# Low and high half of a weight block in one tile, sums of blocks stored in both halves, column sums by transposition, and a ring of 49 tiles

## The chip, the cores and the metric

The kernel runs on one core of a Trainium2 chip. The metric is the device time of one execution in microseconds (us). Before the change it is 2611.89 us, the median of three runs (2609.43 to 2612.32).

## The reference, cut to what matters

One layer is computed for 2112 tokens (2048 of a prompt, 64 of a sample with states of their own), model width 1024, all in float32.

```python
h = rms_norm(x, g_pre)
vA, bA, cA, zA, q, f, iv, zB, gA, gB = split_cols(h @ w_in)        # 1024 x 10240
u_ext = concat([conv_hist, cA * vA])
yA = (silu(zA) * bA * causal_conv3(u_ext, conv_w)) @ w_a_out       # path A
fg = lb + (1 - lb) * sigmoid(f)                                    # path B: 8 heads, chunks of 64
S_new, o = hgrn2_scan(S0, silu(q) * K_B**-0.5, 1 - fg, iv, log(fg))
o = o * rsqrt(mean(o * o) + EPS)
yB = (o * g_onorm * silu(zB)) @ w_b_out
out = (sigmoid(gA) * yA + sigmoid(gB) * yB) @ w_o
x = x + rms_norm(out, g_post)
x = x + (p @ w_ple_proj) * sigmoid(rms_norm(x, g_ple) @ w_ple_gate)
```

## The kernel before, in words

**Blocks.** Tokens are worked on in three blocks of 704, each in two halves of 352, which is the moving size of nearly every matmul. Features lie on partitions. For each block the program runs `path_b` (eight heads of the scan with their four in-projections), `path_a` (the convolution path), the merge with W_A and W_B, W_O, the norms and the gate W_G. Products that belong to the next block fill gaps.

**Split floats.** A float32 operand is split in a high part `hi` (a cast on ScalarE) and a low part `lo = x - hi` (a subtraction on VectorE), both in `split` at L188. A product is three matmuls: hi with the high part of the tokens, hi with their low part, lo with their high part (L363, L364, L365 in `sgroup`; L496 to L498 in `in_turn`; L529 to L531 in `mm3`).

**Weights.** A weight comes in blocks of 128x512 floats (256 KB, `w_blk`). SyncE (SP) loads a block into one of 5 `raw` tiles (L198). The first time a block is used, ScalarE casts and VectorE subtracts (L188), and SP stores the low part to DRAM (`low`, L225). Later, ScalarE casts again (L218), and SP loads the stored low part (L219) into one of 4 `lo` or 3 `s` tiles. There are 4 `hi` tiles.

**Seven products for eight.** Large products are done as groups of 2x2 blocks with seven products (`PRODUCTS`, `sgroup`); four of the seven weight operands are sums of blocks, S1 to S4. In block 0 `combined` makes them on VectorE (L297) in an `s` tile and stores the sum (L276) and its low part (L225). From block 1 on `kept_w` loads a sum into `raw`, casts it, and loads its low part. The sums of the late weights are made ahead by `prepare_sums`: GpSimd (POOL) loads four blocks into ring tiles (L320), VectorE makes four sums (L337, L339, L341, L343), POOL stores each sum (L326); each is split by a cast and a subtraction, and POOL stores the low part (L329). For W_A and W_B this runs in block 0's merge (`ahead=True`, eight groups, the low part through the three `s` tiles); for W_O in block 1 and for W_G in block 2 it runs a group at a time beside `path_a`.

**Order.** Program order with priorities sets each engine's order; tiles come from pools in turn, and who takes a tile waits for all readers of the one that lay there, a storing DMA too. `hooks` is a list of small pieces of work; one is taken after each product of a group. Column sums: `col_rstd` adds 128 rows of squares by matmuls with a column of ones (L620), three tiles of a half; VectorE scales them (L591), POOL takes the power (L593), `spread` turns the result back by transposing matmuls (L604). The ring has 52 tiles of 128x708 floats for everything else.

Of the kernel before, what the change touches and what calls it, by code (L numbers as in the profile page):

```python
# [35 lines left out]
CUT = 1344  # L36
BN = 704
HN = BN // 2
NB = TOK // BN
RING = 52  # L40
# [5 lines left out]
def plan():  # L46


    out = []
    for t0 in range(0, TOK, BN):  # L50
        runs, groups = [], []
        for lo, hi, sample in ((0, CUT, False), (CUT, CUT + DEC, True), (CUT + DEC, TOK, False)):
            a, b = max(lo, t0) - t0, min(hi, t0 + BN) - t0
# [7 lines left out]
        halves = [dict(t0=t0 + o, off=o, n=HN) for o in (0, HN)]  # L61
        out.append(dict(t0=t0, n=BN, runs=runs, npair=npair, parts=parts, groups=groups, segs=halves, last=t0 + BN == TOK))
# [20 lines left out]
def hybrid_step(  # L83
# [35 lines left out]
    def rt(n=BN, dt=F32):  # L119
        t = ring.tile([P, BN + 4], dt, tag="r", name=nm("r"))  # L120
        return t if n is None else t[:, :n]

    def hf(n=HN):
        return ring.tile([P, HN + 32], F32, tag="hf", name=nm("hf"), bufs=HALVES)[:, :n]
# [4 lines left out]
    def ps_gemm():  # L129
        return psg.tile([P, 512], F32, tag="pg", name=nm("pg"))[:, :HN]  # L130

    def spill(kind, j):
        return dram.tile([P, BN], F32, tag=f"{kind}{j}", name=nm(kind), bufs=2)
# [4 lines left out]
    ones = const.tile([P, 1], F32, tag="ones", name="ones")  # L138
    V.memset(ones, 1.0)
# [6 lines left out]
    keep = const.tile([P, BN], F32, tag="keep", name="keep")  # L146
    atts = [
        const.tile([P, max(len(b["parts"][i]) for b in blocks), P], F32, tag=f"att{i}", name=f"att{i}") for i in range(NPART)
# [41 lines left out]
    def split_rt(src):  # L190
        hi, lo = rt(dt=F32R), rt(dt=F32R)
# [3 lines left out]

    def load_raw(src):
        raw = wp.tile([P, 4, P], F32, tag="raw", name=nm("raw"), bufs=5)
# [3 lines left out]
    lows, turn = {}, [0]  # L201

    def low_tile():

        turn[0] += 1
        if turn[0] % 7 in (1, 3, 5):
            return sum_tile(F32R)
        return wp.tile([P, 4, P], F32R, tag="lo", name=nm("lo"))

    def sum_tile(dt=F32):  # L210
        return wp.tile([P, 4, P], dt, tag="s", name=nm("s"), bufs=3)

    def split_w(raw, key=None, queue=SP):

        hi = wp.tile([P, 4, P], F32R, tag="hi", name=nm("hi"))
        if key in lows:
            lo = low_tile()
            A.copy(hi, raw)  # L218
            SP.dma_start(lo.bitcast(F32), lows[key])  # L219
            return hi, lo  # L220
        lo = wp.tile([P, 4, P], F32R, tag="lo", name=nm("lo"))
        split(raw, hi, lo)
        if key is not None:
            lows[key] = dram.tile([P, 4, P], F32, tag=f"lo{key}", name=nm("low"), bufs=1)
            queue.dma_start(lows[key], lo.bitcast(F32))  # L225
        return hi, lo

    def load_w(idx, anew=False):

        parts = []  # L230
        for half_ in range(2):
            raw = load_raw(w_blk[idx, half_])
            with tc.high_priority():
                unread = W_A <= idx < W_O and (idx % KB < KH or half_ == 0)
                parts.append(split_w(raw, None if anew or unread else (idx, half_)))
# [37 lines left out]
    def keep_sum(name, i1, s, queue):  # L273

        sums.setdefault(i1, {})[name] = dram.tile([P, 4, P], F32, tag=f"{name}_{i1}", name=nm(name), bufs=1)
        queue.dma_start(sums[i1][name], s)  # L276
        return split_w(s, (i1, name), queue)

    def kept_w(i1, i2, name, anew=False):

        keys = dict(A11=(i1, 0), A12=(i1, 1), A22=(i2, 1))
        if name in keys:
            return split_w(load_raw(w_blk[keys[name]]), None if anew else keys[name])
        return split_w(load_raw(sums[i1][name]), (i1, name))

    def combined(i1, i2, first):

        queue = SP if first else G
        with tc.high_priority():
            if not first and i1 in sums:  # L290
                return {n: kept_w(i1, i2, n) for _, n, _, _, _ in PRODUCTS}
            a11, a21, a22, a12 = (load_raw(w_blk[i, h]) for i, h in ((i1, 0), (i2, 0), (i2, 1), (i1, 1)))
# [16 lines left out]
    def prepare_sums(firsts, ahead):  # L309
# [4 lines left out]
        def tile_of(dt=F32):  # L314
            return rt(4 * P, dt).rearrange("p (k c) -> p k c", c=P)

        def load(i1, i2):
            out = [tile_of() for _ in range(4)]
# [4 lines left out]
        def keep(name, i1, s):  # L323
            sums.setdefault(i1, {})[name] = dram.tile([P, 4, P], F32, tag=f"{name}_{i1}", name=nm(name), bufs=1)
            lows[i1, name] = dram.tile([P, 4, P], F32, tag=f"lo{name}_{i1}", name=nm("low"), bufs=1)
            G.dma_start(sums[i1][name], s)  # L326
# [6 lines left out]
        for n, (i1, _) in enumerate(groups):  # L333
# [4 lines left out]
            keep("S1", i1, a22)  # L338
            V.tensor_tensor(a21, a11, a21, ALU.subtract)  # L339
            keep("S3", i1, a21)  # L340
            V.tensor_tensor(a11, a22, a11, ALU.subtract)  # L341
            keep("S2", i1, a11)
            V.tensor_tensor(a12, a12, a11, ALU.subtract)  # L343
# [5 lines left out]
    def sgroup(i1, i2, hc, sink, first, mid=None, by_k=False):  # L349
# [5 lines left out]
        def product(n, ks):  # L355
# [3 lines left out]
            hi, lo = w[block]  # L359
# [34 lines left out]
    def half(t, h):  # L394
        return t[:, h * HN : (h + 1) * HN]
# [15 lines left out]
    def plain_group(i1, i2, hs, sink, raws=None, between=None):  # L411
# [14 lines left out]
        def add(c, ks):  # L426
            for k in ks:
                hi, lo = w[c, k // KH]
# [41 lines left out]
    def in_turn(stages, operand):  # L470
# [10 lines left out]
        for i, (st, n) in enumerate(todo):  # L481
# [3 lines left out]
            for g in range(KH):  # L485
                i1, i2 = st["idx"] + g, st["idx"] + KH + g
                with tc.high_priority():
                    hi, lo = kept_w(i1, i2, IN_TURN[n][0], IN_TURN[n][0] in st["anew"])
# [37 lines left out]
    def mm3(ps, w, act, k, c, ks=range(KB)):  # L526
        hi, lo = w[k // 4]
# [19 lines left out]
    def gemm_late(idxs, act, segs, late):  # L547
# [3 lines left out]
        ks = [k for k in range(KB) if k != late] + [late]  # L551
# [55 lines left out]
    def spread_all(cols):  # L607

        rs = rt()
        for h in range(2):  # L610
            A.copy(half(rs, h), spread(cols[h], HN))
        return rs

    def col_rstd(acc, n):
# [3 lines left out]
        with placed():  # L618
            for i, o in tiles_of(n):
                T.matmul(pc[:, i : i + 1], acc[:, o : o + P], ones, start=True, stop=True)  # L620
        rstd_of(pc[:, : cols.shape[1]], cols, 1.0 / D)
# [19 lines left out]
    def load_x(bl, k):  # L641
        t = rt()
        G.dma_start(t, x_fm[k * P : (k + 1) * P, bl["t0"] : bl["t0"] + BN])
        return t

    def row_rstd(bl, out):

        out.extend(cols_tile(HN) for _ in bl["segs"])
        todo = [(cols, s["t0"] + o, i) for cols, s in zip(out, bl["segs"]) for i, o in tiles_of(HN)]
# [120 lines left out]
    def path_a(bl, hc, a, first, extra, ready=None):  # L770

        for j in range(KB):
            next(extra, None)
            n = bl["n"]
            pos = [r[0] + 2 * i for i, r in enumerate(bl["runs"])]
            hists = [hist_s if r[2] else hist_p for r in bl["runs"]]
            ct, u, conv = rt(), rt(None), rt()
# [4 lines left out]
            def times_u(h, v):  # L782
                for (o, ln, _), q in zip(bl["runs"], pos):
                    lo, hi = max(o, h * HN), min(o + ln, (h + 1) * HN)
                    if lo < hi:
                        V.tensor_tensor(
                            u[:, q + 2 + lo - o : q + 2 + hi - o], v[:, lo - h * HN : hi - h * HN], ct[:, lo:hi], ALU.mult
# [13 lines left out]
            for (o, ln, _), q, hist in zip(bl["runs"], pos, hists):  # L801
                d = conv[:, o : o + ln]
                A.mul(d, u[:, q : q + ln], cw[0][:, j : j + 1])
                for w in (1, 2):
                    V.scalar_tensor_tensor(d, u[:, q + w : q + w + ln], cw[w][:, j : j + 1], d, ALU.mult, ALU.add)
# [20 lines left out]
    def head_prep(bl, hc, hd, first, hs):  # L826
        n, npair = bl["n"], bl["npair"]
        nch, np1 = n // CH, npair * P
# [18 lines left out]
        qc = small.tile([P, 2, BN // CH], F32, tag="qc", name=nm("qc"))  # L847
        f, r = qc[:, 0, :nch], qc[:, 1, :nch]
        ka, kb, qx, vt, z = hf(HN + 32), rt(), rt(), rt(), rt()

        def scaled(after):
# [16 lines left out]
            two = kb[:, : 4 * P].rearrange("p (c q t) -> p c q t", q=4, t=CH)  # L868
            rest = kb[:, 4 * P : np1].rearrange("p (g c t) -> p g c t", c=2, t=CH)[:, :, 0, :]
# [632 lines left out]
```

## Time and profile before

| | |
|---|---|
| median of three runs | 2611.89 us |
| the profiled execution's own time | 2611.61 us |
| its span | 2609.9 us |
| granted TensorE clock, mean | 1.000 |
| TensorE (PE) busy | 2588.6 us, 99% |
| VectorE (DVE), ScalarE (ACT), GpSimd (POOL) busy | 64%, 59%, 15% |
| DMA queue of SP (q1), of POOL (q0), share of 16 engines | 65.4%, 17.0% |

Busy shares are means over the whole span. The waits of an engine name the instruction that waited and what released it. A window of the trace gives the busy time of each engine and the share of the 16 DMA engines in that stretch.

### The profile page before, as it was taken

The numbers are of one execution on the slowest core, as the hardware profiler recorded it, in microseconds if no ns is written. First come the engines' busy times: TensorE is split into PE (matmuls) and PEld (weight loads), VectorE is DVE, ScalarE is ACT, GpSimd is POOL, SyncE is SP. The second block draws the span as 40 slices with busy tenths as digits, with TensorE's granted clock in tenths as the row PEclk, the third lists the DMA queues.
The fourth block names the chain that finished last, engine by engine and source line by source line (L and its number), as shares of the span: only waits on it lengthen the run. The fifth ranks groups of instructions, "written<-read, shape, count | busy, mean of one in ns | idle before, by whom it ended". The sixth has DMA issues, their size and how long they took to land.

```text
span 2609.9 us, 47443 instructions
## 1 busy us (share of the span) xinstructions
PE 2588.6 (99%) x16562; PEld 2572.5 (99%) x16562; DVE 1667.1 (64%) x3232; ACT 1538.9 (59%) x2940; POOL 392.6 (15%) x722
## 2 busy tenths in 40 slices
PE   8999999999999999999999999999999999999999
PEld 8999999999999999999999999999999999999998
DVE  8778888888766555455545568553455544568756
ACT  6666665554434644677745556466667744555746
POOL 2000000200441212101112211021000101210220
PEclk9999999999999999999999999999999999999999
DMA  7687787898988997777789989599776789999977
GB/s 285 234 275 259 251 285 257 306 318 286 342 292 285 351 320 259 248 231 224 226 288 359 381 311 312 193 359 358 229 230 220 224 256 335 377 321 309 339 256 240
DMA packets 362672, 745.99 MB, mean 286 GB/s; under 512 B 44640, under 2 KB 49280, under 8 KB 362432
## 3 DMA queue, kind: packets, MB, share of 16 engines
q1 hardware_dynamic: 319680, 579.55, 65.4%
q0 software_dynamic: 42464, 163.37, 17.0%
q8 instruction: 130, 2.13, 0.3%
q14 instruction: 110, 0.90, 0.1%
q10 hardware_dynamic: 288, 0.05, 0.0%
HBM read 531.74 MB, written 211.04 MB: 285 GB/s over the span
## 4 chain that ended last, share of the span: by engine, by line
PE 89%; DMA 3%; DVE 2%; issue 2%; ACT 1%; POOL 1%; DVEq 0%; POOLq 0%; ACTq 0%; SPq 0%
PE pg L363 19%; PE pg L365 19%; PE pg L364 19%; PE pg L496 4%; PE pg L497 4%; PE pg L498 4%; PE pg L530 4%; PE pg L531 4%; PE pg L529 4%; PE pa L994 1%; PE pa L958 1%; PE pa L996 1%; PE pa L944 1%; DMA r<-w_blk 1%; DMA raw<-S 1%
## 5 line engine op out<-in xcount | busy, mean ns | idle before, releaser
L363 PE MATMUL pg<-r,hi 128*128 128x352 f32 x3304 | 1092.9, 331 | 4.6 <-DVE r L409 3.1
L364 PE MATMUL pg<-r,hi 128*128 128x352 f32 x3304 | 1067.6, 323 | 0.0
L365 PE MATMUL pg<-r,lo 128*128 128x352 f32 x2356 | 762.1, 323 | 1.2 <-DMA lo<-low 1.2
L218 ACT CAST hi<-raw 128x512 fp32r<-128x512 f32 x720 | 445.0, 620 | 499.8 <-PE pg L364 165.6
L363 PEld LDWEIGHTS pg<-r,hi 128*128 128x128 f32 x3304 | 622.2, 188 | 9.1 <-DVE r L409 3.2
L364 PEld LDWEIGHTS pg<-r,hi 128*128 128x128 f32 x3304 | 622.2, 188 | 0.0
L365 PEld LDWEIGHTS pg<-r,lo 128*128 128x128 f32 x2356 | 442.3, 188 | 1.8 <-DMA lo<-low 1.7
L365 PE MATMUL pg<-r,s 128*128 128x352 f32 x948 | 306.2, 323 | 0.1
L530 PE MATMUL pg<-r,hi 128*128 128x352 f32 x768 | 248.4, 324 | 0.0
L529 PE MATMUL pg<-r,hi 128*128 128x352 f32 x768 | 248.1, 323 | 0.0
L188 ACT CAST hi<-raw 128x512 fp32r<-128x512 f32 x218 | 134.6, 621 | 153.1 <-PE pg L364 53.5
L188 DVE TENSOR_TENSOR r<-r,r 128x352 fp32r<-128x352 f32 (+3 forms) x298 | 182.8, 637 | 62.7 <-ACT r L188 61.7
L497 PE MATMUL pg<-r,hi 128*128 128x352 f32 x672 | 217.3, 325 | 0.0
L496 PE MATMUL pg<-r,hi 128*128 128x352 f32 x672 | 213.6, 325 | 0.1
L531 PE MATMUL pg<-r,lo 128*128 128x352 f32 x656 | 211.9, 323 | 0.1
L188 ACT CAST r<-r 128x352 fp32r<-128x352 f32 (+3 forms) x298 | 162.2, 580 | 56.9 <-DVE r L1114 15.4
L188 DVE TENSOR_TENSOR lo<-raw,hi 128x512 fp32r<-128x512 f32 x218 | 149.4, 687 | 63.5 <-ACT hi L188 55.2
L365 PEld LDWEIGHTS pg<-r,s 128*128 128x128 f32 x948 | 178.4, 188 | 0.4 <-DMA s<-low 0.4
L188 ACT CAST hi<-s 128x512 fp32r<-128x512 f32 x160 | 98.5, 621 | 123.0 <-PE pg L364 105.8
L377 ACT COPY hf<-pg 128x352 f32<-128x352 f32 x354 | 157.1, 446 | 11.5 <-PE pg L365 10.9
L530 PEld LDWEIGHTS pg<-r,hi 128*128 128x128 f32 x768 | 144.3, 188 | 0.3 <-DVE r L188 0.2
L529 PEld LDWEIGHTS pg<-r,hi 128*128 128x128 f32 x768 | 144.2, 188 | 0.0
(367 smaller groups left out, 4157.0 us busy)
## 6 DMA issues: line engine op xcount, KB each, us to landing
raw<-w_blk SPq DMA_DIRECT2D x570, 256.0 KB, 4.2
lo<-low SPq DMA_DIRECT2D x411, 256.0 KB, 4.4
raw<-S SPq DMA_DIRECT2D x408, 256.0 KB, 4.4
low<-lo SPq DMA_DIRECT2D x314, 256.0 KB, 3.7
s<-low SPq DMA_DIRECT2D x309, 256.0 KB, 4.2
S<-s SPq DMA_DIRECT2D x152, 256.0 KB, 3.2
r<-w_blk POOLq DMA_DIRECT2D x64, 256.0 KB, 7.3
S<-r POOLq DMA_DIRECT2D x64, 256.0 KB, 5.8
```

The source lines that it names most:

```text
L188: return A.copy(hi, src).ins, V.tensor_tensor(lo, src, hi.bitcast(F32), ALU.subtract).ins
L218: A.copy(hi, raw)
L363: add(hi[:, k, :], xhi, start=start and k == 0, stop=False)
L364: add(hi[:, k, :], xlo, start=False, stop=False)
L365: last[0] = add(lo[:, k, :], xhi, start=False, stop=k == KH - 1).ins
L377: copied = A.copy(got[n], ps[bank])
L496: add(hi[:, k, :], xhi, start=start and k == 0, stop=False)
L497: add(hi[:, k, :], xlo, start=False, stop=False)
L498: last[0] = add(lo[:, k, :], xhi, start=False, stop=k == KH - 1).ins
L529: T.matmul(ps, hi[:, k % 4, :], xhi[:, c], start=k == ks[0], stop=False)
L530: T.matmul(ps, hi[:, k % 4, :], xlo[:, c], start=False, stop=False)
L531: last[0] = T.matmul(ps, lo[:, k % 4, :], xhi[:, c], start=False, stop=k == ks[-1]).ins
```

## The change

1. A weight block has one tile for both halves (`both`, tag `w`, 7 of them, 512 KB each); the tags `hi`, `lo` and `s` are gone. There are 6 `raw` tiles for 5.
2. A sum is stored with both halves side by side (512 KB, `sum_home`) and loaded by one DMA straight into a `w` tile. The cast of a sum that was loaded again is gone.
3. Where `s` tiles held sums, `raw` tiles do now: in `combined` the sum itself, in `prepare_sums` with `ahead` the high and the low part of each sum.
4. `prepare_sums` in blocks 1 and 2 runs in four pieces that are put among the hooks; high and low part lie in ring tiles.
5. `col_rstd` transposes the three tiles of squares and adds along the free axis on VectorE, in place of the matmuls with ones.
6. The ring has 49 tiles. The first head of block 0 gets one more empty hook. `gemm_late` takes the k steps in a rotated order, the norms' steps are one hook apart from where they were, the last block's two halves share tiles and full-width loads of x, and `final_gate` works half by half.
7. Sizes of blocks are read from a table, `SIZES`; with (704, 704, 704) the tiling is what it was.

```diff
-RING = 52
+RING = 49
+WEIGHTS = 7
+RAWS = 6
...
-        raw = wp.tile([P, 4, P], F32, tag="raw", name=nm("raw"), bufs=5)
+    def raw_tile(dt=F32):
+        return wp.tile([P, 4, P], dt, tag="raw", name=nm("raw"), bufs=RAWS)
+    def both():
+        return wp.tile([P, 2, 4, P], F32R, tag="w", name=nm("w"), bufs=WEIGHTS)
...
-        hi = wp.tile([P, 4, P], F32R, tag="hi", name=nm("hi"))
-        if key in lows:
-            lo = low_tile()
-            A.copy(hi, raw)
-            SP.dma_start(lo.bitcast(F32), lows[key])
-            return hi, lo
-        lo = wp.tile([P, 4, P], F32R, tag="lo", name=nm("lo"))
-        split(raw, hi, lo)
+        t = both()
+        split(raw, t[:, 1], t[:, 0])
...
-        return split_w(load_raw(sums[i1][name]), (i1, name))
+        t = both()
+        SP.dma_start(t.bitcast(F32), sums[i1][name])
+        return t
...
             def total(name, x, y, op):
-                s = sum_tile()
+                s = raw_tile()
                 V.tensor_tensor(s, x, y, op)
-                out[name] = keep_sum(name, i1, s, queue)
+                out[name] = split_w(s)
+                queue.dma_start(sum_home(name, i1), out[name].bitcast(F32))
                 return s
...
         def keep(name, i1, s):
-            sums.setdefault(i1, {})[name] = dram.tile([P, 4, P], F32, tag=f"{name}_{i1}", name=nm(name), bufs=1)
-            lows[i1, name] = dram.tile([P, 4, P], F32, tag=f"lo{name}_{i1}", name=nm("low"), bufs=1)
-            G.dma_start(sums[i1][name], s)
-            lo = sum_tile(F32R) if ahead else tile_of(F32R)
-            split(s, lo, lo)
-            G.dma_start(lows[i1, name], lo.bitcast(F32))
+            home = sum_home(name, i1)
+            hi, lo = (raw_tile(F32R) if ahead else blocks_of(F32R) for _ in range(2))
+            split(s, hi, lo)
+            G.dma_start(home[:, 1], hi.bitcast(F32))
+            G.dma_start(home[:, 0], lo.bitcast(F32))
...
-        ks = [k for k in range(KB) if k != late] + [late]
+        ks = [(late + 1 + k) % KB for k in range(KB)]
...
-                T.matmul(pc[:, i : i + 1], acc[:, o : o + P], ones, start=True, stop=True)
-        rstd_of(pc[:, : cols.shape[1]], cols, 1.0 / D)
+                T.transpose(pc[:, i * P : i * P + P], acc[:, o : o + P], ident)
+        nt = cols.shape[1]
+        V.tensor_reduce(cols, cols3(pc, nt), axis=mybir.AxisListType.X, op=ALU.add)
+        rstd_of(cols, cols, 1.0 / D)
...
                 if step == 2:
-                    hooks.append(None)
+                    hooks.extend([None] * (2 if first and hd == 0 else 1))
...
-                if j >= 3:
+                if j == 3:
                     next(sums_, None)
+                elif j > 3 and not first:
+                    hooks.extend([partial(next, sums_, None), None, None] * 4)
...
-            spread_out((norm, (0, 1, 0, 1) + (0, 1, 0) * KB + (0, 1, 0, 1) + (0, 1) * KB))
+            spread_out((norm, (0, 1, 0, 0, 1) + (0, 1, 0) * (KB - 1) + (0, 1) + (0, 1, 0, 0, 1) + (0, 1) * KB))
```

Three places in the order of instructions follow. The first is SP's order in block 0's merge, where it loads the blocks of W_A and W_B into `raw` tiles. DMASW is the completion of a DMA that POOL issued, DMAHW of one that SP issued. Before:

```order
620 L198 DMA raw_8979<-w_blk 128x512 [waits DMAHW6_49,DVE_49]
621 L198 DMA raw_8985<-w_blk 128x512 [waits DMAHW7_49,DVE_49]
622 L198 DMA raw_9051<-w_blk 128x512 [waits DMAHW1_49,DMAHW0_49,DVE_49]
623 L198 DMA raw_9057<-w_blk 128x512 [waits DMAHW3_49,DVE_49]
624 L198 DMA raw_9165<-w_blk 128x512 [waits DMAHW5_49,DMAHW2_49,DVE_49]
```

With the change:

```order
468 L226 DMA raw_8395<-w_blk 128x512 [waits DMAHW6_49,DMASW7_49,DVE_49]
469 L226 DMA raw_8400<-w_blk 128x512 [waits DMAHW7_49,DMASW0_49]
470 L226 DMA raw_8465<-w_blk 128x512 [waits DMAHW0_49,DMAHW1_49,DMASW1_49,DVE_49]
471 L226 DMA raw_8470<-w_blk 128x512 [waits DMAHW3_49,DMASW2_49]
...
473 L226 DMA raw_8577<-w_blk 128x512 [waits DMASW4_49,DMASW3_49,DVE_49]
```

Where a load waited for VectorE's subtraction of an earlier block, it now waits as well for a store on POOL's queue, since the tile that it takes held half a sum.

The second place is on SP in block 1's `path_b`, where blocks and sums that were stored in block 0 are loaded again. Before, one group of seven operands is loaded by

```order
701 L198 DMA raw_11082<-S_562_2297 128x512 [waits DMAHW7_49,Activation_49]
702 L219 DMA s_11079<-low_2293 128x512 [waits DMAHW0_49,PE_49]
703 L198 DMA raw_11088<-S_567_2307 128x512 [waits DMAHW1_49,Activation_49]
704 L219 DMA lo_11085<-low_2303 128x512 [waits DMAHW2_49,PE_49]
705 L219 DMA s_11091<-low_2313 128x512 [waits DMAHW3_49,PE_49]
706 L198 DMA raw_11094<-S_572_2317 128x512 [waits DMAHW4_49,Activation_49]
```

With the change the same stretch of a group reads

```order
551 L226 DMA raw_10721<-w_blk 128x512 [waits DMAHW1_49,Activation_49]
552 L305 DMA w_10438<-S_488_2201 128x1024 [waits DMAHW2_49,PE_49]
553 L305 DMA w_10440<-S_491_2208 128x1024 [waits DMAHW3_49,PE_49]
554 L305 DMA w_10442<-S_494_2215 128x1024 [waits DMAHW4_49,PE_49]
555 L226 DMA raw_10732<-w_blk 128x512 [waits DMAHW5_49,Activation_49]
```

A sum and its low half, two loads and a cast, have become one load of 128x1024 that waits for TensorE alone, the reader of the `w` tile.

The third place is TensorE in the first head of block 0, where the head's normalised output is transposed (L1008, L1044 with the change) between two products. Before:

```order
666 L365 MATMUL pg_1492<-r_656,lo_1447 128x352
667 L363 MATMUL pg_1686<-r_384,hi_1628 128x352
668 L364 MATMUL pg_1686<-r_384,hi_1628 128x352
669 L1008 MATMUL pa_1612<-ident,r_1529 128x128 x4
670 L365 MATMUL pg_1686<-r_384,lo_1629 128x352
```

With the change:

```order
666 L393 MATMUL pg_1439<-r_652,w_1394 128x352
667 L391 MATMUL pg_1612<-r_384,w_1569 128x352
668 L392 MATMUL pg_1612<-r_384,w_1569 128x352
...
678 L393 MATMUL pg_1612<-r_454,w_1569 128x352
679 L1044 MATMUL pa_1627<-ident,r_1476 128x128 x4
680 L391 MATMUL pg_1633<-r_552,w_1576 128x352
```

The four transposes stood behind two matmuls of the product and now stand behind all twelve.

More of the change, by code (lines that the diff above doesn't have):

```diff
@@ L60, in plan @@
         parts = [groups[i : min(i + 4, npair)] for i in range(0, npair, 4)] + [[g] for g in groups[npair:]]
-        halves = [dict(t0=t0 + o, off=o, n=HN) for o in (0, HN)]
-        out.append(dict(t0=t0, n=BN, runs=runs, npair=npair, parts=parts, groups=groups, segs=halves, last=t0 + BN == TOK))
+        halves = [dict(t0=t0 + o, off=o, n=n // 2) for o in (0, n // 2)]
+        out.append(dict(t0=t0, n=n, runs=runs, npair=npair, parts=parts, groups=groups, segs=halves, last=t0 + n == TOK))
+        t0 += n
     return out
@@ L117, in nm, with width_of, of_block, rt @@
         return f"{s}_{uid[0]}"
[L119 to L124, printed above, removed]
+    wide = [blocks[0]["n"]]
+    @contextmanager
+    def width_of(bl):
+        before, wide[0] = wide[0], bl["n"]
+        try:
+            yield
+        finally:
+            wide[0] = before
+    def of_block(bl, gen):
+        while True:
+            with width_of(bl):
+                try:
+                    next(gen)
+                except StopIteration:
+                    return
+            yield
+    def rt(n=None, dt=F32):
+        return ring.tile([P, BMAX + 4], dt, tag="r", name=nm("r"))[:, : n or wide[0]]
+    def hf(n=None):
+        return ring.tile([P, HMAX], F32, tag="hf", name=nm("hf"), bufs=HALVES)[:, : n or wide[0] // 2]
     def ps_attn():
@@ L1197, in final_norm @@
         for j in range(KB):
-            fetch()
+            fetch(ahead + j + 1)
             xj = xo[j][:, c]
@@ L1347, in hybrid_step @@
     with behind_all((*done, *copies)):
-        cols = [col_rstd(half(acc, h), HN) for h in range(2)]
+        cols = [col_rstd(half(acc, h), wide[0] // 2) for h in range(2)]
         ph, done = split_p(ph1)
```

242 lines of the change are left out of this document (128 added, 114 removed).

## The prediction

> **What bounds the kernel now.** I read the busy shares first, then the waits of TensorE, then single stretches. The page:
>
> ```profile
> span 2609.9 us, 47443 instructions
> PE 2588.6 (99%) x16562; PEld 2572.5 (99%) x16562; DVE 1667.1 (64%) x3232; ACT 1538.9 (59%) x2940; POOL 392.6 (15%) x722
> L218 ACT CAST hi<-raw 128x512 fp32r<-128x512 f32 x720 | 445.0, 620 | 499.8 <-PE pg L364 165.6
> raw<-S SPq DMA_DIRECT2D x408, 256.0 KB, 4.4
> ```
>
> TensorE is busy for 99% of the span. The change leaves its large matmuls as they are, so nothing that it saves on ScalarE or on queues shows in the time unless TensorE waited for it. The headline saving is large and off the path: 408 of the casts at L218 go with the 408 reloads of a sum, 408 x 0.62 us = 253 us of an engine that is 59% busy and waits itself, for TensorE above all. What can be won is in the list of TensorE's waits, all of them:
>
> ```profile
> engine line waited for: us in total, times, longest us
> PE pa L1058 <- ACT r L188: 6.6, 1, 6.6
> PE pg L363 <- DVE r L409: 3.1, 9, 0.6
> PE pa L1008 <- DVE r L1003: 1.7, 1, 1.7
> PE pg L363 <- ACT hi L218: 1.5, 2, 0.7
> PE pg L365 <- DMA lo<-low: 1.2, 1, 1.2
> PE pa L1058 <- ACT r L1065: 0.9, 2, 0.6
> PE pa L1060 <- DVE r L188: 0.2, 1, 0.2
> ```
>
> The rows of L1058 and L1060 are the start (7.7 us until first tokens and weights are there), which the change leaves alone. The other four rows hold 7.5 us: that is the whole of the waiting to be won, 0.3% of the time. I reckon against the profiled execution, 2611.61 us (the span and 1.7 us around it); the median, 2611.89, is 0.3 us above it.
>
> **The change part by part.**
>
> *First head.* The 1.7 us row is one wait of the transposes at L1008 for VectorE's scaling. The order with the change puts ten matmuls of the product ahead of them that stood behind. What a matmul takes is seen in a stretch without waits:
>
> ```profile
> core 0: us, PE busy (x), PEclk, DMA share, GB/s
> 655.00:670.00 15.00, 15.00 (x95) 1.00 0.71 249
> 670.00:685.00 15.00, 15.00 (x95) 1.00 1.01 370
> 685.00:700.00 15.00, 15.00 (x96) 1.00 0.99 371
> ```
>
> 15 us / 95 = 0.158 us a matmul, so the transposes come 1.6 us later and the wait all but goes: **-1.6**. What is late next is a wait of the rest, 0.1 us.
>
> *Sinks.* The nine waits for L409 fall in two places: between 140 and 620 us (path_b of block 0, where VectorE makes sums ahead of the addition that frees a product), and after 1300 us, beside `prepare_sums`.
>
> ```profile
> PE pg L363 <- DVE r L409: 1.5, 6, 0.3
> PE pg L363 <- DVE r L409: 1.6, 3, 0.6
> DVE r L337 <- DMA r<-w_blk: 51.3, 10, 8.7
> ```
>
> The first row is the early stretch. There the addition stands earlier in VectorE's order against the chain behind it with the change, by more than the 0.3 us that a wait lasts: **-1.5**. The second row is the late one, the third is VectorE standing before a sum until its blocks have landed, up to 8.7 us. The pieces put other work between the sums, but the first piece of a group still meets loads that were issued a piece earlier. I take a third of the 1.6: **-0.5**; the ends are -1.6 and, if every one of the eight groups of blocks 1 and 2 waits like the worst now (0.6), 8 x 0.6 - 1.6 = +3.2.
>
> *Casts and low halves.* The two waits for L218 come in the first group of the merges of blocks 1 and 2, where four `hi` tiles keep a cast from running ahead; with seven `w` tiles it has three products more, 3 x 12 x 0.158 = 5.7 us, against 0.7: **-1.5**. The wait for a low half (1.2) lies at 898 us, in a stretch where landings are slow:
>
> ```profile
> raw<-S SPq DMA_DIRECT2D x14, 256.0 KB, 8.0
> lo<-low SPq DMA_DIRECT2D x14, 256.0 KB, 7.5
> ```
>
> One load of 512 KB takes the place of these two. No row has its landing. From below it is the 8.0 of its larger half; from above the two in a row, 15.5; I take 8.0 plus 256 KB at the rate of 371 GB/s above, 0.7, so 8.7 us. A `w` tile is asked for again six products ahead, 6 x 12 x 0.158 = 11.4 us, which covers it: **-1.0**, with the ends -1.2 and, at 15.5 us in the three or four such groups of a merge, 4 x 4.1 - 1.2 = +15.
>
> *Column sums.*
>
> ```profile
> L620 PE MATMUL pa<-ones,r 128*128 128x1 f32 x84 | 10.1, 244 | 0.1
> L604 PE MATMUL pa<-ident,cols 128*128 128x128 f32 x54 | 7.8, 273 | 0.0
> L1001 DVE TENSOR_REDUCE ms<-r 128x4 f32<-128x512 f32 x24 | 16.5, 686 | 30.5 <-ACT r L1000 30.5
> ```
>
> 42 matmuls (14 halves of three tiles) leave two records each and hold TensorE for 10.1 us. A transpose leaves one and holds it for 7.8 / 54 = 0.144 us; 42 of them take 6.1: **-4.0**. VectorE adds 14 reductions of at most 0.69 us. Where `spread` comes hooks later they are hidden by the products between; at the start, where the power is what `spread` waits for, one pair shows: **+0.7** (0 to 1.4).
>
> So far: -1.6 - 1.5 - 0.5 - 1.5 - 1.0 - 4.0 + 0.7 = **-9.4**.
>
> *Raw tiles in block 0's merge.* This is the part that can cost. Two steps of a merge are 96 matmuls, 96 x 0.158 = 15.2 us, and in them one group of sums is made. Before, a group needs four raw tiles of five for blocks, and four `s` tiles of three for low halves; no load of a block waited for a store. Now blocks and halves of sums share six raw tiles: 4 + 8 = 12 a group, so each tile has to go round twice in 15.2 us, once as half a sum, until POOL's store has landed, and once as a block, from its load until it is split (or both times as sums). The rows between 650 and 800 us:
>
> ```profile
> raw<-w_blk SPq DMA_DIRECT2D x38, 256.0 KB, 6.6
> S<-r POOLq DMA_DIRECT2D x32, 256.0 KB, 6.0
> low<-s POOLq DMA_DIRECT2D x32, 256.0 KB, 5.4
> ...
> L188 ACT CAST hi<-raw 128x512 fp32r<-128x512 f32 x40 | 24.6, 621 | 27.8 <-PE pg L530 16.9 <-issue 6.0 <-PE pg L364 3.5
> L188 ACT CAST s<-r 128x512 fp32r<-128x512 f32 x32 | 19.8, 622 | 38.9 <-DMA low<-s 15.7 <-DVE r L341 6.8 <-DVE r L339 5.5
> L188 DVE TENSOR_TENSOR lo<-raw,hi 128x512 fp32r<-128x512 f32 x40 | 27.5, 687 | 14.9 <-ACT hi L188 12.9 <-DMA low<-lo 1.8
> L326 POOL DMA_DIRECT2D S<-r x32 | 17.4, 545 | 48.4 <-DVE r L337 40.8 <-issue 3.0 <-DMA low<-s 1.7
> ```
>
> One round trip: cast 0.62, subtraction 0.69, POOL's issue 0.54, landing 6.0, load 6.6, cast 0.62, subtraction 0.69 = 15.8 us, 0.6 over the 15.2. In the busiest stretch, 675 to 695 us, and in a lighter one, 760 to 800 us, the landings are
>
> ```profile
> S<-r POOLq DMA_DIRECT2D x5, 256.0 KB, 6.4
> raw<-w_blk SPq DMA_DIRECT2D x4, 256.0 KB, 7.5
> ...
> S<-r POOLq DMA_DIRECT2D x9, 256.0 KB, 4.8
> raw<-w_blk SPq DMA_DIRECT2D x8, 256.0 KB, 6.0
> ```
>
> which give 3.16 + 13.9 = 17.1 us and 3.16 + 10.8 = 14.0 us. So eight groups cost from nothing to 8 x 1.9 = 15 us, and by the median 8 x 0.6 = 4.8. The row of the casts of blocks says that a block now waits for TensorE (16.9 us of its 27.8), so it is early; and seven `w` tiles are 3.5 steps of look-ahead where four `hi` were 2, 1.5 x 7.6 = 11 us more, which takes up most of a shortfall of 4.8. I take a third of it: **+1.6**.
>
> By the page "DMA: Bandwidth & Descriptors" of the Trainium skill, section "Anatomy of one DMA — SWDGE (gpsimd) path", a DMA from POOL takes about 2.0 us and its bytes at 436 GB/s, 2.6 us for 256 KB. By that the store leaves the round trip at 12.4 us and the merge costs nothing: 2602.2 us, as an estimate. The trace disagrees for this stretch: 5.4 and 6.0 us, since the queues are full (share 1.01 at 670 to 685 us).
>
> *The rest* (the rotated k order, half-wise gate, shared tiles of the last block, 49 ring tiles) I set at nothing: TensorE has no wait in the list that belongs to it. Three ring tiles fewer can make a load later; the ends are 0 and one landing, 6.6 us.
>
> **Sum**: 2611.6 - 9.4 + 1.6 = 2603.8, about **2604 us**.
>
> **The rivals.**
>
> *Raw tiles bind (slower).* Place: block 0's merge, 660 to 800 us. It decides from the point where store and load landings together exceed 15.2 - 3.2 = 12.0 us. For it: the median row gives 12.6, half of the stretches more; ScalarE's order mixes casts of sums, which wait for a tile, with casts of blocks behind them, so that a late store holds a block too; ScalarE already stands 15.7 us for three `s` tiles. Against it: the stores are spread out by the very wait, and the 4.8 us of the lighter stretch would do. Price: 1.9 us in each group and about 3 before the first blocks that take such a tile, 18 us, so 2611.6 - 9.4 + 18 = 2620; with another 1.5 us a group for work standing behind a late cast, 2632.
>
> The Trainium skill, page "Perfetto Trace Analysis", section "Identifying Performance Opportunities", says that the same gap coming back on the engine that should be full can mean too little memory for the next tile. By that rule this rival would be seen as a gap once every two steps; before, no such row exists in this stretch (all 15.00 us of each window are busy).
>
> *Waits move (no change).* Column sums bring their 3.3 us, but the waits of 0.3 to 1.7 us come back a few matmuls later, and the merge takes 3 to 5: 2611.6 - 3.3 + 3 = 2611. For it: every one of these waits is an engine that is late by a little, and the order only shifts them.
>
> *The pieces and the large loads don't do what they are for (slower).* VectorE meets each late group at a piece between two products, and the 512 KB land as two in a row: +3.2 and +15 on the -7.9 of the other parts (without -0.5 and -1.0, without the merge): 2611.6 - 7.9 + 18 = 2622.
>
> **How the numbers follow.** A measurement of this kernel tells from no change about 0.2%, 5.2 us: faster is below 2606.7, slower above 2617.1. Chances: the forecast 0.50 (its own range 2599 to 2607); raw tiles 0.30, a tenth of that inside the band; waits move 0.14, in the band; pieces and large loads 0.06, slower. Together faster 0.50, same 0.17, slower 0.33. The range begins where the merge is free and all of these waits are gone, 2611.6 - 9.4 - 0.1 - 1.1 - 0.7 - 0.2 = 2600.1, less 2 us for shorter gaps (TensorE is idle for 21.3 us, the list holds 15.2 of them): 2598. It reaches up into the two slower rivals, to 2625, and leaves out the upper part of the raw tiles' case.
>
> **What would show it.** In the profile after: L1008's row of 1.7 us gone; no early row of L409; no wait for casts in the merges of blocks 1 and 2; the transposes at about 0.14 us each, and VectorE's reduce rows. For the raw tiles: windows between 660 and 800 us with TensorE under 15.00 of 15 us, a wait of the merge's matmuls for a cast or subtraction of a block, and SP waiting for POOL's stores. The prediction is wrong if that stretch loses more than 8 us, or if a load of a stored sum appears among TensorE's waits.

## The result and the profile after

The changed kernel takes 2653.48 us (median of four, 2652.42 to 2657.35) against 2611.89 (median of four by then): ratio 1.0164, 95% interval 1.0146 to 1.0182. It is slower by 41.6 us, where 8 us less were forecast; the range ended at 2625. The page of the kernel after has these lines for those shown of before:

```profile
span 2651.2 us, 45772 instructions
PE 2593.8 (98%) x16520; PEld 2572.1 (97%) x16520; DVE 1676.4 (63%) x3267; ACT 1313.4 (50%) x2532; POOL 389.7 (15%) x712
L559 PE MATMUL pg<-r,w 128*128 128x352 f32 x768 | 253.3, 330 | 33.2 <-ACT w L209 33.2
...
w<-S SPq DMA_DIRECT2D x408, 512.0 KB, 4.8
...
S<-raw POOLq DMA_DIRECT2D x64, 256.0 KB, 4.4
```

ScalarE is rid of the casts of reloaded sums (59% to 50% busy), and the time is longer all the same: 33.2 us of waiting stand before L559, the first matmul of each three in the merge (L529 before). All waits of TensorE after:

```profile
PE pg L559 <- ACT w L209: 33.2, 9, 9.2
PE pa L1093 <- ACT r L209: 6.9, 1, 6.9
PE pg L391 <- ACT hf L405: 2.3, 6, 0.5
PE pa L634 <- POOL cols L623: 2.0, 6, 0.4
PE pa L1093 <- ACT r L1100: 1.9, 2, 1.3
PE pg L391 <- DVE r L438: 1.6, 2, 1.4
PE pg L391 <- DMA w<-S: 1.3, 3, 0.8
PE pa L1044 <- DVE r L1039: 0.7, 1, 0.7
PE pa L979 <- DVE att L988: 0.6, 1, 0.6
```

The first row is nine waits for the cast of a block, up to 9.2 us each, and all nine lie between 650 and 835 us: in block 0's merge, the last one at the first product of W_O right behind it. Without that row the list holds 17.7 us (two rows of 0.2 are not shown), and before it held 15.2. The same stretch in windows of 15 us, each of which was full before:

```profile
core 0: us, PE busy (x), PEclk, DMA share, GB/s
655.00:670.00 15.00, 15.00 (x95) 1.00 0.50 169
670.00:685.00 15.00, 13.90 (x85) 1.00 0.88 330
685.00:700.00 15.00, 12.48 (x73) 0.95 0.91 319
...
745.00:760.00 15.00, 7.84 (x49) 0.88 0.35 117
760.00:775.00 15.00, 12.78 (x64) 0.78 0.75 254
...
790.00:805.00 15.00, 7.71 (x48) 0.86 0.55 191
```

Two things are to be seen. In the two windows where TensorE loses most, the DMA engines are far from full (shares 0.35 and 0.55), and from 738 to 752 us, ahead of the longest wait, their share is 0.12: it is not a crowd on the queues. And the granted clock falls below 1.00; before, every window up to 2600 us shows 1.00. SP's waits in the stretch name the new link, first after, then before:

```profile
SPq L226 <- DMA S<-raw: 109.5, 29, 28.7
SPq L237 <- DVE w L209: 46.8, 8, 9.9
```

```profile
SPq L198 <- DVE lo L188: 87.3, 24, 7.8
SPq L225 <- DVE lo L188: 47.6, 19, 9.3
SPq L219 <- DMA low<-s: 5.0, 2, 4.8
```

Loads of blocks (L226) wait 109.5 us for stores of half sums, once 28.7 us. How a store that lands in 4.4 us can hold a load for so long is seen in the order of time around the longest of TensorE's waits (752.9 to 762.0 us). SP's loads:

```profile
729.48 1.10 SPq L226 DMA_DIRECT2D raw<-w_blk  x2
...
756.72 6.35 SPq L226 DMA_DIRECT2D raw<-w_blk  x4
```

ScalarE:

```profile
746.02 0.78 ACT L209 CAST r<-r 128x704 fp32r<-128x704 f32 x1 [9.74 <-DVE r L1149]
747.38 0.78 ACT L209 CAST r<-r 128x704 fp32r<-128x704 f32 x1 [0.58 <-DVE r L1149]
750.46 1.66 ACT L209 CAST raw<-r 128x512 fp32r<-128x512 f32 x3 [2.29 <-DVE r L360]
...
761.38 0.62 ACT L209 CAST w<-raw 128x512 fp32r<-128x512 f32 x1 [4.67 <-DMA raw<-w_blk]
```

VectorE, in the same stretch:

```profile
743.70 1.50 DVE L1148 TENSOR_TENSOR r<-pg,r 128x352 f32<-128x352 f32 x3 [6.69 <-PE pg L561]
...
749.01 0.69 DVE L359 TENSOR_TENSOR r<-r,r 128x512 f32<-128x512 f32 x1
749.73 0.69 DVE L360 TENSOR_TENSOR r<-r,r 128x512 f32<-128x512 f32 x1
...
753.32 0.68 DVE L209 TENSOR_TENSOR raw<-r,raw 128x512 fp32r<-128x512 f32 x1
```

POOL stores that low half:

```profile
754.30 0.54 POOL L351 DMA_DIRECT2D S<-raw  x1 [1.85 <-DVE raw L209]
```

After the two loads that are issued by 731 us, SP's next one is at 756.72. Its tile belongs, in the order in which tiles are given out, to half a sum. VectorE's order has that sum (from 749.0) behind the evacuation of a product (L1148), which waits for TensorE until 743.7. The sum's high half is cast at 750.5, its low half is subtracted at 753.3, and the store of the low half, issued at 754.3, has landed by 756.6. Only then the block is loaded. It is cast at 761.38, when TensorE has stood since 752.9. From the cast of the sum to the landing it is some 6 us; the load stood for the tile for 26. The landing itself was short: between 740 and 760 us these stores land in 2.6 us (median of seven).

### The profile page after: what moved, and what is told of

Read it like the earlier page. It is cut to its first block, busy times and chain, and to the rows that moved or that the text cites. A ratio compares the mean times of both kernels' runs of the same rounds, so it can differ in the third digit from the quotient of the medians.

```text
span 2651.2 us, 45772 instructions
## 1 busy us (share of the span) xinstructions
PE 2593.8 (98%) x16520; PEld 2572.1 (97%) x16520; DVE 1676.4 (63%) x3267; ACT 1313.4 (50%) x2532; POOL 389.7 (15%) x712
## 5 line engine op out<-in xcount | busy, mean ns | idle before, releaser
L391 PE MATMUL pg<-r,w 128*128 128x352 f32 x3304 | 1092.9, 331 | 5.2 <-ACT hf L405 2.3
L392 PE MATMUL pg<-r,w 128*128 128x352 f32 x3304 | 1067.0, 323 | 0.0
L393 PE MATMUL pg<-r,w 128*128 128x352 f32 x3304 | 1066.9, 323 | 0.0
L391 PEld LDWEIGHTS pg<-r,w 128*128 128x128 f32 x3304 | 621.5, 188 | 10.0 <-ACT hf L405 4.1
L392 PEld LDWEIGHTS pg<-r,w 128*128 128x128 f32 x3304 | 623.0, 189 | 0.3
L393 PEld LDWEIGHTS pg<-r,w 128*128 128x128 f32 x3304 | 620.6, 188 | 0.0
L209 ACT CAST w<-raw 128x512 fp32r<-128x512 f32 x384 | 235.6, 620 | 274.9 <-DMA raw<-w_blk 92.6
L246 ACT CAST w<-raw 128x512 fp32r<-128x512 f32 x306 | 189.2, 619 | 294.3 <-issue 96.5
L209 DVE TENSOR_TENSOR w<-raw,w 128x512 fp32r<-128x512 f32 x384 | 263.6, 689 | 106.7 <-ACT w L209 105.6
L559 PE MATMUL pg<-r,w 128*128 128x352 f32 x768 | 253.3, 330 | 33.2 <-ACT w L209 33.2
L405 ACT COPY hf<-pg 128x352 f32<-128x352 f32 x354 | 157.4, 450 | 251.6 <-PE pg L393 251.3
L561 PE MATMUL pg<-r,w 128*128 128x352 f32 x768 | 252.4, 329 | 0.7 <-DMA w<-low 0.2
L560 PE MATMUL pg<-r,w 128*128 128x352 f32 x768 | 251.6, 328 | 0.0
L527 PE MATMUL pg<-r,w 128*128 128x352 f32 x672 | 217.9, 325 | 0.0
L528 PE MATMUL pg<-r,w 128*128 128x352 f32 x672 | 216.2, 323 | 0.0
L526 PE MATMUL pg<-r,w 128*128 128x352 f32 x672 | 214.3, 324 | 0.0
L559 PEld LDWEIGHTS pg<-r,w 128*128 128x128 f32 x768 | 147.3, 192 | 36.4 <-ACT w L209 36.4
L561 PEld LDWEIGHTS pg<-r,w 128*128 128x128 f32 x768 | 146.6, 191 | 3.4 <-DVE w L209 2.8
L560 PEld LDWEIGHTS pg<-r,w 128*128 128x128 f32 x768 | 147.4, 192 | 0.1
L527 PEld LDWEIGHTS pg<-r,w 128*128 128x128 f32 x672 | 126.5, 188 | 2.4 <-DVE r L209 1.5
```

The lines of the kernel that those rows point to most:

```text
L209: return A.copy(hi, src).ins, V.tensor_tensor(lo, src, hi.bitcast(F32), ALU.subtract).ins
L246: A.copy(t[:, 1], raw)
L391: add(hi[:, k, :], xhi, start=start and k == 0, stop=False)
L392: add(hi[:, k, :], xlo, start=False, stop=False)
L393: last[0] = add(lo[:, k, :], xhi, start=False, stop=k == KH - 1).ins
L405: copied = A.copy(got[n], ps[bank])
```

## The experiments

The theory (A) is that loads of blocks wait for raw tiles that are given to sums. The rivals are the queues (B) and the rest of the change (C). A table behind the last experiment has, for most of these kernels, the time of the stretch in question.

**1. Nine raw tiles**

```diff
-RING = 49
+RING = 47
-RAWS = 6
+RAWS = 9
```

> The changed kernel with 9 raw tiles for 6 (ring 47 for 49 to make room). Theory A, tiles taken in program order: in block 0's merge a block's load waits for a tile that holds half a sum, and the sum is made only at its place behind the end of a product; with 9 tiles, 12 a group, the loads run some 4 us x 3 further ahead, so most of the 33 us of TensorE's waits go, and the clock there is 1.00 again: 2605 to 2618. Theory B, queues: the same bytes in the same stretch land too late: 2645 to 2655 as it was. Theory C, the loss is of other parts (ring, order, clock): 2645 or more, since the ring is smaller still.

2642.91 us, ratio 1.0124 (1.0109 to 1.0139). It misses all three: faster than the change by 10 us, far from free. TensorE's waits for casts in the merge fall to 15.2 us in three, SP still waits 68.3 us for stores. The count of tiles counts, but a half more is not enough; 12 tiles are taken in a group.

**2. Three tiles of their own for halves of sums**

```diff
-            hi, lo = (raw_tile(F32R) if ahead else blocks_of(F32R) for _ in range(2))
+            hi, lo = (sum_half() if ahead else blocks_of(F32R) for _ in range(2))
...
+    def sum_half():
+        return wp.tile([P, 4, P], F32R, tag="s", name=nm("s"), bufs=SUMS)
+SUMS = 3
-RING = 49
+RING = 47
```

> The changed kernel, but the two halves of each sum made ahead lie in a pool of three tiles of their own, not in raw tiles (ring 47 for 49 to make room). Theory A: no load of a block waits for a store any more; the merge loses 0 to 6 us where ScalarE stands for one of the three tiles with casts of blocks behind: 2603 to 2611. Theory B: same bytes, 2645 to 2655. Theory C: 2645 or more.

2614.46 us, ratio 1.0014 (1.0005 to 1.0024): 39 us of the 41.6 are gone with the same bytes in the same stretch. B and C fall as causes of the bulk. Windows of this kernel:

```profile
685.00:700.00 15.00, 15.00 (x95) 1.00 0.97 359
...
745.00:760.00 15.00, 15.00 (x95) 1.00 0.90 334
```

TensorE is full at a DMA share of 0.97. The products of W_A and W_B take 123.7 us for 123.4 before the change (160.6 with it): the merge itself is free. It is not the 2603 to 2611 that I expected: at 784 and 804 us, in the products of W_O right behind, there are 5.4 us of new waits (for an operand and for an evacuation). Both stand in order behind a half sum that goes into one of the three tiles: at 783 us VectorE stands 3.0 us before one, at 801 us ScalarE 3.8 us for a store from such a tile. That is the loss of 0 to 6 us that the expectation names.

**3. Halves of sums in ring tiles**

```diff
-            hi, lo = (raw_tile(F32R) if ahead else blocks_of(F32R) for _ in range(2))
+            hi, lo = (blocks_of(F32R) for _ in range(2))
```

> The changed kernel, but the two halves of each sum made ahead lie in ring tiles, as they do in blocks 1 and 2. Theory A: 2602 to 2610 if the 49 ring tiles suffice; where they don't, loads of the merge's other operands wait and 5 to 15 us come back. Theory B and C: 2645 to 2655.

2616.24 us, ratio 1.0021 (1.0012 to 1.0030). The second answer by another way. The foreseen shortage is there: 3.4 us of waits for an evacuation at 769 and 788 us, where VectorE stands 4.1 and 2.8 us for the load of a gate into a ring tile.

**4. The kernel before with low halves in raw tiles**

```diff
-            lo = sum_tile(F32R) if ahead else tile_of(F32R)
+            lo = wp.tile([P, 4, P], F32R, tag="raw", name=nm("raw"), bufs=5) if ahead else tile_of(F32R)
```

> The kernel before with one part of the change alone: in its sums made ahead the low half lies in a raw tile (5 of them, 4 + 4 taken in a group) and not in an s tile. Theory A: loads of blocks wait for stores here too, TensorE waits in the merge, the clock falls: 2625 to 2655. Theory B (queues of the new stores) and C (other parts): 2610 to 2615, nothing changes.

2645.80 us, ratio 1.0135 (1.0119 to 1.0150). One line of the change, put alone into the kernel before, costs 35 us. Its waits:

```profile
PE pg L529 <- ACT hi L188: 16.3, 5, 4.6
...
PE pg L531 <- DVE lo L188: 1.2, 2, 0.8
```

17.5 us of waits go with a span of 2641.8 us, 31.9 more; most of the rest goes with the clock (below), which is 0.77 between 700 and 720 us.

**5. Sums called for earlier, tiles shared as in the change**

```diff
         for j, pss in enumerate(gemms(W_B, ob, segs)):
+            if j in (0, 2, 4, 6, 7):
+                next(extra, None)
             fetch(GB, j + 1)
...
-            if j in (0, 2, 4, 6, 7):
-                next(extra, None)
```

(and the same for W_A)

> The changed kernel, raw tiles shared as they are, with one thing moved: in block 0's merge a group of sums is called for ahead of the evacuation of a step's product in program order, not behind it. Theory A1 (what holds a tile is the wait of the sum for its place, behind a product's end): the sums come up to 7 us earlier, TensorE waits for less than half of 33 us, 2615 to 2635. Theory A2 (what holds it is the cast, store and landing by their durations): 2645 to 2655, within 5 us of what it was.

2637.25 us, ratio 1.0103 (1.0089 to 1.0116). 16 us come back without a tile or a byte changed, just short of A1's range, and TensorE waits 17.7 us in the merge for 33.2, a little over the half that A1 names:

```profile
PE pg L559 <- ACT w L209: 10.1, 6, 3.4
PE pg L559 <- DVE r L1150: 7.0, 1, 7.0
```

The waits for casts fall to less than a third; the second row is new, an evacuation that now stands in VectorE's order behind subtractions of late blocks. So the place of the sum behind a product's end is part of what holds a tile (A1), and not all of it.

**6. Low half over its sum, 6 w tiles, 5 raw, 3 of their own, ring 49**

```diff
-            hi, lo = (raw_tile(F32R) if ahead else blocks_of(F32R) for _ in range(2))
+            hi = sum_half() if ahead else blocks_of(F32R)
+            lo = s.bitcast(F32R)
...
-WEIGHTS = 7
-RAWS = 6
+WEIGHTS = 6
+RAWS = 5
+SUMS = 3
```

> The changed kernel with a sum's low half written over the sum in its ring tile, and its high half in one of three tiles of its own; 5 raw and 6 w tiles make room, the ring stays at 49. Four turns over three tiles a group, as before the change. Theory A: no waits in the merge, the clock stays at 1.00, and what is left is the rest of the change: 2604 to 2611. If the rest is what keeps the second and third experiment at 2614 to 2616: 2612 to 2618.

2624.39 us, ratio 1.0053 (1.0040 to 1.0065), a miss. The merge is nearly full, but one w tile less is paid elsewhere:

```profile
PE pg L396 <- DMA w<-S: 4.5, 9, 1.0
PE pg L566 <- DMA w<-low: 4.2, 1, 4.2
```

That is the late large load of the prediction's last rival; with seven w tiles these loads cost 1.5 us. A further 5.5 us are six waits for an evacuation in block 0's `path_b`. The run has one raw tile less too, and which tile costs which wait is not shown.

**7. Column sums by transposition, alone in the kernel before**

```diff
-                T.matmul(pc[:, i : i + 1], acc[:, o : o + P], ones, start=True, stop=True)
-        rstd_of(pc[:, : cols.shape[1]], cols, 1.0 / D)
+                T.transpose(pc[:, i * P : i * P + P], acc[:, o : o + P], ident)
+        nt = cols.shape[1]
+        V.tensor_reduce(cols, cols3(pc, nt), axis=mybir.AxisListType.X, op=ALU.add)
+        rstd_of(cols, cols, 1.0 / D)
```

> The kernel before with the column sums by transposition alone. By the prediction's term: 4.0 us of matmuls less, 0.7 more at the start, 2607 to 2609. By the profile of the change, where spread now waits for POOL's power six times (2.0 us): 2609 to 2611.

2611.20 us, ratio 1.0000 (0.9991 to 1.0009). The matmuls are shorter as reckoned, and two new rows of waits stand against that:

```profile
PE pa L604 <- POOL cols L593: 2.0, 5, 0.6
...
PE pa L620 <- DVE r L641: 0.7, 1, 0.7
```

**8. One empty hook more in the first head, alone in the kernel before**

```diff
-                    hooks.append(None)
+                    hooks.extend([None] * (2 if first and hd == 0 else 1))
```

> The kernel before with the one empty hook more in the first head alone. By the prediction's term the wait of 1.7 us goes: 2609.5 to 2610.5. If the hook only moves the wait to the pieces behind it: 2611 to 2612.

2609.03 us, ratio 0.9993 (0.9984 to 1.0002). The row of 1.7 us is gone from the profile; the difference of 2 us fits but isn't told from none by the times.

**9. Low half over its sum, 8 turns over 6 raw tiles**

```diff
-            hi, lo = (raw_tile(F32R) if ahead else blocks_of(F32R) for _ in range(2))
+            hi = raw_tile(F32R) if ahead else blocks_of(F32R)
+            lo = s.bitcast(F32R) if ahead else blocks_of(F32R)
```

> The changed kernel with the low half of a sum made ahead written over the sum in its ring tile, so that only high halves take raw tiles: 4 + 4 turns a group over 6 tiles instead of 8 + 4. Refined theory A (a block's load waits for the tile taken as many turns before as there are tiles; where that is half a sum of the same group, it waits until that sum is made, cast and stored): two of four blocks of a group stand behind a sum of their own group, not all four: some waits stay in the merge, 2615 to 2635, clock under 1.00 there. Rival (it is the number of bytes that POOL stores, or the rate of turns): below 2612, since 8 turns over 6 tiles are fewer than before had for its raw tiles and its s tiles together.

2627.12 us, ratio 1.0063 (1.0049 to 1.0076). Four turns fewer bring 26 us; some waits stay, as refined A has it, and the rival's time below 2612 did not come.

**10. As the ninth, 8 raw tiles and ring 47**

```diff
-RING = 49
-RAWS = 6
+RING = 47
+RAWS = 8
```

> As the ninth, with 8 raw tiles for the 8 turns of a group (ring 47 to make room). Refined theory A: a block's load waits for a tile of the group before, which is long stored: no waits of SP for stores of its own group, the merge is full and its clock 1.00; what is left is the ring's: 2608 to 2616. Rival (sharing as such, or the pace of the stores): within 10 us of the ninth.

2630.57 us, ratio 1.0078 (1.0063 to 1.0094). A miss, and the time that the rival named: as many tiles as turns do not free the merge. TensorE still waits 10.3 us there, and SP's loads of blocks still 39.3 us for stores. The order of time before the first wait shows why. SP:

```profile
727.43 2.74 SPq L226 DMA_DIRECT2D raw<-w_blk  x4
```

and ScalarE:

```profile
722.91 0.62 ACT L209 CAST w<-raw 128x512 fp32r<-128x512 f32 x1 [0.78 <-PE pg L562]
741.17 0.78 ACT L209 CAST r<-r 128x704 fp32r<-128x704 f32 x1 [17.63 <-DVE r L1150]
...
751.68 2.18 ACT L209 CAST w<-raw 128x512 fp32r<-128x512 f32 x4
```

The four blocks are asked for in time, at 727, but ScalarE's order has their casts behind casts of an operand and of sums that wait, by way of VectorE, for a product's end; it stands 17.6 us and casts the blocks at 751.7, while TensorE waits from 747.9.

**11. The kernel before with three small parts**

The edits of the seventh and eighth, and:

```diff
-            spread_out((norm, (0, 1, 0, 1) + (0, 1, 0) * KB + (0, 1, 0, 1) + (0, 1) * KB))
+            spread_out((norm, (0, 1, 0, 0, 1) + (0, 1, 0) * (KB - 1) + (0, 1) + (0, 1, 0, 0, 1) + (0, 1) * KB))
```

> The kernel before with three small parts of the change: column sums by transposition, the norms' steps one hook later (which gives the longer chain of a column sum its time), one empty hook more in the first head; tiles as before. By the profiles of the seventh and eighth: 2.0 us of waits of spread mostly gone, 4.0 us of matmuls and 1.7 us of the first head saved, 0.7 lost at the start: 2605 to 2608. If waits only move: 2609 to 2611.

2608.73 us, ratio 0.9991 (0.9982 to 1.0000), the lowest median of the study and hardly told from the kernel before. The hook later does not give spread its time: its row of waits is 2.3 us in five.

**12. The tenth with the fifth's edit**

```diff
+            if j in (0, 2, 4, 6, 7):
+                next(extra, None)
             fetch(GB, j + 1)
...
-            if j in (0, 2, 4, 6, 7):
-                next(extra, None)
```

> The tenth kernel (8 raw tiles for 8 turns of a group) with the fifth's edit: a group of sums is called for ahead of the evacuation of a step's product. Theory P (what is left in the tenth is order: casts of blocks that have landed stand on ScalarE behind casts of sums and operands that wait for a product's end): TensorE's waits in the merge fall from 10 us to under 6, 2616 to 2625. Theory T (sharing as such, or the smaller ring): 2628 to 2633, as the tenth.

2617.15 us, ratio 1.0020 (1.0010 to 1.0029). With tiles enough and the sums ahead of the product's evacuation, TensorE's waits in the merge are two of 0.9 us together. Raw tiles are still shared and SP still waits 26.5 us for stores: sharing as such is not what costs. What is left of this kernel's distance stands elsewhere, among it

```profile
PE pa L1094 <- ACT r L1101: 3.7, 2, 3.1
PE pa L1045 <- DVE ms L622: 2.6, 1, 2.6
```

in the first 140 us, where the change itself has 1.9 and 0.7. It is not the smaller ring alone: experiment 2, with the same 47 ring tiles and 6 raw tiles, has 1.8 and 0.7 there, and experiments 1 and 10, with 9 and 8 raw tiles, have more too. Why more raw tiles go with it is open.

All kernels run the same 1152 matmuls of W_A, W_B and W_O in block 0 (L529 to L531; L559 to L561 in the change). The time from the first of them to the last, and the rest of the span, in us, from one trace of each kernel:

| kernel | the stretch | the rest |
|---|---|---|
| before | 186.1 | 2423.8 |
| the change | 232.5 | 2418.7 |
| 1: nine raw tiles | 215.9 | 2431.3 |
| 2: three tiles of their own | 193.5 | 2422.2 |
| 3: ring tiles | 193.7 | 2423.1 |
| 4: before, low halves in raw tiles | 216.6 | 2425.2 |
| 5: sums earlier | 215.8 | 2418.7 |
| 6: six w tiles, five raw | 187.3 | 2436.8 |
| 9: eight turns, six raw tiles | 204.5 | 2421.6 |
| 10: eight turns, eight raw tiles | 202.1 | 2427.1 |
| 12: the tenth, sums earlier | 187.4 | 2428.1 |

The change lost 46.4 us in the stretch and won 5.1 outside it. Experiment 12 takes back 45 of the 46.4. The times of the kernel before lie between 2608.42 and 2614.43 us over all the runs, so a difference of a few us in the right-hand column says little.

## Why the prediction was wrong, point by point

**Raw tiles in block 0's merge** is the step that failed. The place, the link (a load that waits for POOL's store), what would show it, and the sign of the rival were right; the price was not, 1.6 us in the sum and 18 in the rival, where the stretch lost 46.4. Two things were left out.

First, the round trip of a tile was made of work and landings only, 15.8 us, and held against 15.2. In the trace the store lands in 4.4 us, not 6.0, and the load in 7.2, not 6.6 (medians between 650 and 830 us): by durations the trip would have been 1.0 us shorter than reckoned. But a tile is given out in program order, and the time in which it is reserved for a sum that is not yet made belongs to the trip. The sum's place is behind a product's end on VectorE, and blocks' casts stand behind the sums' on ScalarE; the rival names that order, but no term prices it. So the look-ahead of seven w tiles, which I counted as cover, was empty at these waits: the loads that fill it wait for something that TensorE has to do first. The runs show both halves: experiments 2 and 3 (no shared tile) end all but some 7.5 us of it, 5 (earlier place) takes 16 us, 10 (more tiles alone) does not end it, 12 (tiles and place) does.

Second, a wait of TensorE was priced at its own length. Around the longest:

```profile
752.00:754.00 2.00, 0.84 (x6) 1.00 0.70 262
...
762.00:764.00 2.00, 1.95 (x6) 0.50 0.92 238
764.00:766.00 2.00, 2.00 (x8) 0.50 1.02 411
766.00:768.00 2.00, 1.82 (x9) 0.83 1.03 414
768.00:770.00 2.00, 2.00 (x15) 1.00 0.26 99
```

From 762 to 768 us TensorE is busy 5.77 us and starts 23 matmuls; at 0.158 us they take 3.6. The wait costs 2.1 us more than itself. The trace has five waits above 2 us (2.5, 2.5, 9.2, 8.1 and 7.9), and the clock is at 0.50 after each of them. Of the 46.4 us that the stretch lost, 33.2 are waits and 13.2 are more than the waits, 2.6 for each of the five if all of it is theirs. The span grew by 41.3, so the rest of the change is worth about -5.1 in this trace, not -9.4.

The Trainium skill, page "TensorE: Matmul & The Clock Gate", section "Part 1: The HAM clock gate (the "warmup" mystery)", gives the array two states, half and full clock, and about 3.4 us of activity before it is let up again. The trace agrees: rows of 0.50 and 1.00, and 3 to 5 us of slow matmuls after each of the five waits. I had not put that page beside the rival; it would have raised its price.

**The start**, set at nothing: its three rows went from 7.7 to 9.0 us. What in the change makes them longer is not shown.

**First head**: -1.6 forecast; the row went from 1.7 to 0.7, and alone it is gone. Right, near enough.

**Sinks**: the early six are gone (-1.5), a wait of 0.6 for a mask took a place among them; the late three of 1.6 us became two of 1.6. -1.5 right, -0.5 wrong.

**Casts and low halves**: the waits for L218 and for the low half are gone, and in their place stand 2.3 us for L405 and 1.5 us for loads of a sum and of a low half. The gain of 2.5 did not come; this is the rival of waits that move. A load of a stored sum among TensorE's waits (1.3 us) was one of the two signs of being wrong.

**Column sums**: 42 transposes hold TensorE for 6.0 us,

```profile
L650 PE MATMUL pa<-ident,r 128*128 128x128 f32 x42 | 6.0, 272 | 0.0
```

as the 6.1 reckoned, so -4.1 of matmuls. But the longer chain is seen at six places (2.0 us before L634), not only at the start, where I had 0.7; alone it measures as nothing. I had taken it that products between hide the reduction; it did not, for `spread` now waits for POOL's power, which comes behind it.

**The sum of the rest**: the rows named here add up to -1.6, the trace says -5.1; the 3.5 us between are in no row. The fifth experiment's trace, with the same tiles, has -5.1 too, those of 2 and 3, with other tiles, -1.6 and -0.7. So the rest was worth about half of what I gave it, or less. By -5.1, a kernel with the merge free would have come out at 2606.5 us, at the edge of the band of no change; no run shows such a kernel.

What is not settled: how the 46 us part among tile, place and ScalarE's order one by one, since experiments 5, 9 and 10 each change more than one wait; and which of the moves in the rest makes which of the small new waits.

## What to carry to other kernels

A tile that is shared by a look-ahead load and by work done at a place of its own in the program ties the load to that place: count from when the tile is given out, not from when it is used, and ask whether the bottleneck engine has to finish something before the tile can come free. Cover that is counted in buffers is cover only if the loads that fill it wait for nothing that lies behind the bottleneck. A wait of the matrix engine of some two microseconds or more can cost two microseconds more than it lasts (below).

## What the runs showed of the hardware that was not expected

The granted clock fell to 0.50 in the change after single waits of 2.5 to 9.2 us and came back after 3 to 5 us of matmuls; after waits of 1.0 and 1.2 us (679 and 780 us) it did not fall. There is no sharp threshold in these traces: it fell after a wait of 1.8 us in the fifth experiment (812 us) and did not after waits of 2.6 us in the second (784 us) and the tenth (132 us). It fell after every wait of 2.7 us or more behind the start. In the fourth experiment 17.5 us of waits in the merge came with a span 31.9 us longer. A load of 512 KB lands in 4.8 us (median of 408), where the loads of 256 KB of a sum and of a low half that it replaced took 4.4 and 4.2 to 4.4: doubling the bytes added about 0.4 us to the median.
